# Twelve of 22 inner tiles of a down projection by seven products instead of eight

## The chip, the cores and the metric

The kernel runs on one core of a Trainium2 chip. The core has a matmul engine (TensorE, PE in the profile, with its weight loads as PEld), a vector engine (DVE), a scalar engine (ACT), GpSimd (POOL), and SyncE (SP), which issues most of the DMA transfers. The metric is the time of one execution on the device in microseconds (us); lower is better. The profile is that of one execution.

## The reference

One layer of a bidirectional encoder over a sequence of 1024 positions and width 1024, everything in float32:

```
h = rmsnorm(x)
proj = h @ w_in                      # glu, q, v, z_f, z_b, og, g_a, g_b
a = silu(layernorm(dwconv31(glu))) @ pw_w
o = bidirectional gated scan of q, v, z_f, z_b (8 heads, chunks of 64)
b = (rmsnorm_per_head(o) * norm_w * silu(og)) @ o_w
x = x + (sigmoid(g_a) * a + sigmoid(g_b) * b) @ w_out
h2 = rmsnorm(x)
gate, val = split(h2 @ w_up)         # 1024 -> 2 x 2816
g = silu(dwconv3(gate)) * val
x = x + g @ w_down                   # 2816 -> 1024
out = rmsnorm(x)
```

The change is mostly in `g @ w_down`: 2816 inner channels are 22 tiles of 128. Two other places are touched: the product with `sigmoid(g_a)`, and the last residual addition.

## The kernel before

Activations lie transposed, channels on the 128 partitions and positions along the row, in two halves of 512 positions. So a tile is 128x512 and its products go to one PSUM bank (three banks `mm`, two `sc`, two `tr`, one `ob`). A float32 product is made of three matmuls on float32r parts: `split` (L124) makes the high part by an ACT cast and the low part by a DVE subtraction, and `mm3` (L148 to L150) multiplies high by high, high by low and low by high. So each weight page and each activation tile has to pass through ACT and DVE before PE can use it. Activation parts lie in pages `hx` (32), `hy` and `gx` (16 each), weight parts in `wp` (4 pages) and `wq` (3).

There are two kinds of matmul job. `std_job` takes one column of 128 outputs, loads its raw weights, splits them, and for each half of the sequence accumulates all inner tiles in one `mm` bank, which an `evac` function empties. `pair_job` takes two output columns and two halves as a 2x2 block product and forms it by seven products (Strassen's scheme) instead of eight: sums of weight quadrants and sums of activation quadrants are made first, the products 1, 2, 6, 7, 5, 4, 3 run in this order, products 6, 5 and 3 accumulate on the bank of product 1, product 4 on that of product 7, and three banks in between are copied out by ACT (`copy`, L396). The in-projection and the FFN's up projection go by `pair_job` already. The up projection is 22 such jobs, one for each inner tile: column j of the gate and column j of the value. Its weight sums are made by accumulating DMAs that POOL issues.

The FFN after a job: `evac` (L1561 to L1569) combines products into gate and value; `gated` (L1543 to L1556) does the three-tap convolution, the silu and the product with the value, and stores the tile to DRAM as `d_g[j][half]`. The down projection then reads `d_g` back into `ev` and `tm` tiles, splits them (`load_g`), and goes through the 22 inner tiles in groups of 4, 4, 5, 5 and 4: for each group eight `std_job`s, one for each output column. The first group's evictions copy to the accumulators `xr` (16 tiles, ACT, L1690); the next three add to them (DVE, `add_evac`, L1696). The last group (`last_jobs`, `final_evac`) also adds the residual: it loads a `d_x2` tile, adds `xr` to it (L1731), adds the bank to that, and then `turn_out` transposes the tile, sums squares and applies the gain, and `scale_out` scales and stores.

Earlier, `d_ga` and `d_gb` (the sigmoid gates) are stored by the in-projection. The pointwise product of the convolution branch is a `std_job` for each column whose eviction is an ACT copy into an `ev` tile (three buffers) that is stored to `d_a` (L753, L754). The output product of the scan has `merge` as its eviction: it loads `d_gb`, `d_ga` and `d_a`, multiplies, adds and splits (L1438 to L1441).

The order of the work: PE's instructions run in program order. The generators yield after every two inner tiles, and `Stream.fill(n)` advances a stage by n such pieces. `later(n, f)` queues a chore that is due n pieces on. For the other engines a planner of the compiler orders instructions, except where `pin` keeps the program's order. Each engine, and SP's queue, then works strictly in its order.

Of the kernel before, what the change touches and what calls it, by code (L numbers as in the profile page):

```python
# [10 lines left out]
F32 = mybir.dt.float32  # L11
# [7 lines left out]
P = 128  # L19
# [12 lines left out]
H = 512  # L32
# [15 lines left out]
def tile_hybrid_encoder(  # L48
# [233 lines left out]
    def pair_job(src0, src1, nk, acts, wpool, pool, evac, su=4, first=False, late=False, now=False, direct=False, columns=1, stored=None):  # L282
# [7 lines left out]
        def steps(w):  # L290
# [4 lines left out]
            def add(o, a):  # L295
                if first:
                    V.tensor_tensor(o, o, a, op=ALU.add)
                elif direct:
                    pin(V.tensor_tensor(o, o, a, op=ALU.add))
                else:  # L300
                    G.dma_start(o, a, accum_op=ALU.add)

# [84 lines left out]
        def run(w):  # L387
# [13 lines left out]
            p1 = copy(row)  # L401
# [3 lines left out]
            u2 = copy(row)  # L405
            yield from product(7, col)
            p7 = copy(col)
# [120 lines left out]
    d_us = [dp.tile([P, 4, ND // 2 * P], F32, name=f"d_us_{n}") for n in range(3)]  # L528

# [519 lines left out]

    def pw_col(i):  # L1050
        return w_cols(conv_pw_w, 0, NCW, i * P)
# [4 lines left out]
    def pw_first():  # L1056
        prep, run = std_job(pw_col(0), NCW, ca_of, store(d_a[0]))
# [8 lines left out]
    rest_jobs += [std_job(pw_col(i), NCW, ca_of, store(d_a[i])) for i in range(1, ND - 2)]  # L1066
    rest_jobs.append(
        duo_job(pw_col(ND - 2), pw_col(ND - 1), NCW, ca_of, store(d_a[ND - 2]), store(d_a[ND - 1]))
# [365 lines left out]
    def merge(i):  # L1434
        def evac(half, acc):
            sb, sa, a = ev(), ev(), tmp()
            for t, src in ((sb, d_gb), (sa, d_ga), (a, d_a)):
                nc.sync.dma_start(t, src[i][half])  # L1438
            V.tensor_tensor(a, a, sa, op=ALU.mult)
# [53 lines left out]

    h2 = {i: [] for i in range(1, 8)}
# [42 lines left out]
    def ffn_job(j):  # L1537
        val = [None, None]

        def gated(hf):  # L1540
            o, g = hf * H, gp[j % 2]
# [14 lines left out]
            nc.sync.dma_start(d_g[j][hf], val[hf])  # L1556

        def evac(e, half, x0, x1=None, op=None):
# [4 lines left out]
            g = gp[j % 2]  # L1563
# [18 lines left out]
            now=j == 0,  # L1582
            stored=sums_of(d_us[j], ND // 2) if j < len(d_us) else None,
# [75 lines left out]
    groups = [4, 4, 5, 5, 4]  # L1659
    landing = itertools.cycle([ev] * 3 + [tmp] * 4)  # L1660
    gs, jobs = [], []

    def load_g(f, half):

        t = next(landing)()
        nc.sync.dma_start(t, d_g[f][half])
        while len(gs) <= f:
            gs.append([None, None])

        def parts():  # L1670
            gs[f][half] = split(g_page(), g_page(), t, V, True)

        return parts

    s_ffn.fill(14 * (NF - 1) - s_ffn.count)
    for f in range(groups[0]):
# [9 lines left out]
    xr = [[page(fd, "xr", 2 * ND) for _ in range(2)] for _ in range(ND)]  # L1686

# [6 lines left out]
    def add_evac(i):  # L1694
        def f(half, acc):
            V.tensor_tensor(xr[i][half], acc, xr[i][half], op=ALU.add)  # L1696

        return f

    def down_jobs(f0, n, evac):  # L1700
        return [
            std_job(
                w_cols(ffn_w_down, f0 * P, n, i * P), n, lambda k, half: gs[f0 + k][half], evac(i)
            )
            for i in range(ND)
        ]

    def last_jobs(f0, evac):
# [3 lines left out]
        def job(i, half):  # L1712
# [7 lines left out]
            return prep, std_job(None, 4, lambda k, h: gs[f0 + k][h], evac(i), (half,), 1)[1]  # L1720
# [16 lines left out]
    def turn_out(i, half):  # L1737

        t = xr[i][half]
        if i == 0:  # L1740
            out_sum.append(fd.tile([P, ND, 4], F32, tag="os", name=nm("os"), bufs=2))
            out_y.append(fd.tile([P, 4, D], F32, tag="y", name=nm("y"), bufs=2))
        ss, y = out_sum[half], out_y[half]
# [3 lines left out]
        for c in range(4):  # L1747
            junk = fd.tile([P, P], F32, tag="oj", name=nm("oj"), bufs=2)
            A.activation(
                junk, b[:, c * P : (c + 1) * P], AF.Square, accum_out=ss[:, i, c : c + 1]  # L1750
# [23 lines left out]
    def scale_out(half, c):  # L1774
# [12 lines left out]
    out_sum, out_y, out_r = [], [], []  # L1787
    fnw = fd.tile([P, D], F32, name="fnw")
    f0 = 0
    nc.sync.dma_start(  # L1790
        fnw, bass.AP(tensor=final_norm_w.tensor, offset=final_norm_w.offset, ap=[[0, P], [1, D]])
    )
    for n, group in enumerate(groups):
        last = n == len(groups) - 1
        if last:
            st = Stream(run_jobs(last_jobs(f0, final_evac)))
            st.fill(4 * ND + 3)
            finish(0)
            st.drain()
            advance_chores(1 << 10)  # L1800
            finish(1)
        else:
            st = Stream(run_jobs(down_jobs(f0, group, add_evac if n else first_evac)))
            st.fill(12)
            for f in range(f0 + group, f0 + group + groups[n + 1]):
                for half in range(2):
                    later(4, load_g(f, half))
                    st.fill(2)
            st.drain()
            advance_chores(1 << 10)  # L1810
        f0 += group
# [33 lines left out]
```

## Time and profile before

| | us |
|---|---|
| median of 3 runs | 1760.56 |
| lowest and highest | 1758.67, 1764.92 |
| profiled execution | 1763.45 |
| its span | 1761.7 |
| PE busy | 1727.4 (98%) |
| DVE busy | 1207.7 (69%) |
| ACT busy | 808.8 (46%) |
| POOL busy | 156.3 (9%) |

The span is the time from the first to the last recorded instruction; the execution's own time is 1.75 us longer. The stages, by the start of their instructions: in-projection and convolution up to about 480 us, the rest of the in-projection and the scan up to about 830, pointwise product up to about 900, scan output and merge up to about 980, `w_out` up to about 1070, up projection up to about 1505, down projection from there (its first eviction starts at 1508.7, the last one of the fourth group at 1700.0), last group and final norm to the end.

In rows of groups, the part after the bar is busy time, mean ns of one, then the time that the engine was idle just before, and what ended it. In rows of the timeline: start, duration, engine, line, operation, tiles, and in brackets the idle time before with its releaser. In rows of windows: the window, its length, busy time of each engine, the granted clock of PE (1.00 is full speed), the busy share of the DMA engines, and GB/s. Matmul records overlap: the time from one to the next is shorter than the duration of one.

### The profile page before, as it was taken

The page shows a single profiled execution, that of the slowest core. Times are in us where ns is not written, and L with a number is a line of the kernel's source. Part 1 is how long each engine was busy: PE and PEld are TensorE (multiplying, and loading weights), DVE is VectorE, ACT ScalarE, POOL GpSimd, SP SyncE. Part 2 cuts the span into 40 slices and gives each one's busy share as a digit, 9 for nine tenths or more (in the row PEclk, how much of TensorE's full clock was granted, in tenths as well). Part 3 has the DMA queues.
Part 4 walks back from the last instruction along what each step waited for, and adds up shares of the span by engine and source line. Part 5 has one row for each costly group of instructions (what it writes and reads, how often), then busy time and mean ns, then how long its engine had stood idle before and what let it go on. Part 6 is the DMA issues. An engine that isn't in the chain of part 4 may idle for free. (4 is left out here: it accounts for less than half of the span.)

```text
span 1761.7 us, 30307 instructions
## 1 busy us (share of the span) xinstructions
PE 1727.4 (98%) x11878; PEld 1421.6 (81%) x11878; DVE 1207.7 (69%) x1845; ACT 808.8 (46%) x1518; POOL 156.3 (9%) x168
## 2 busy tenths in 40 slices
PE   8999999999999999999999999999999999999997
PEld 6878888887888788888878787888888888888885
DVE  5599999646678878887366566766676667444455
ACT  7444443334476677776542345443443344422223
POOL 2201111100000000000000002111111111000000
PEclk9999999999999999999999999999999999999999
DMA  8778878855663433435489765667766775534233
GB/s 286 241 164 190 195 180 210 201 146 188 207 194 107 122 116 119 140 107 195 127 264 293 229 207 186 159 146 150 152 147 145 148 143 144 160 100 126 73 92 137
DMA packets 333413, 292.33 MB, mean 166 GB/s; under 512 B 24526, under 2 KB 251606, under 8 KB 333270
## 3 DMA queue, kind: packets, MB, share of 16 engines
q1 hardware_dynamic: 281558, 255.78, 46.6%
q0 software_dynamic: 42496, 33.56, 13.4%
q10 hardware_dynamic: 9216, 1.05, 0.4%
q8 instruction: 93, 1.52, 0.4%
q14 instruction: 50, 0.41, 0.1%
HBM read 192.55 MB, written 79.95 MB: 155 GB/s over the span
## 5 line engine op out<-in xcount | busy, mean ns | idle before, releaser
L148 PE MATMUL mm<-hx,wp 128*128 128x512 f32 x1144 | 457.1, 400 | 3.0 <-ACT tm L799 1.7
L150 PE MATMUL mm<-hx,wp 128*128 128x512 f32 x1144 | 446.9, 391 | 2.1 <-DVE wp L124 2.0
L149 PE MATMUL mm<-hx,wp 128*128 128x512 f32 x1144 | 445.9, 390 | 0.0
L124 ACT CAST wp<-wr 128x1024 fp32r<-128x1024 f32 (+2 forms) x171 | 162.1, 949 | 360.2 <-PE mm L149 204.4
L150 PEld LDWEIGHTS mm<-hx,wp 128*128 128x128 f32 x1144 | 214.7, 188 | 50.6 <-DVE wp L124 4.8
L148 PEld LDWEIGHTS mm<-hx,wp 128*128 128x128 f32 x1144 | 214.9, 188 | 49.6 <-DVE ev L748 2.4
L149 PEld LDWEIGHTS mm<-hx,wp 128*128 128x128 f32 x1144 | 215.1, 188 | 42.2 <-issue 0.7
L124 DVE TENSOR_TENSOR wp<-wr,wp 128x1024 fp32r<-128x1024 f32 (+2 forms) x169 | 185.9, 1101 | 87.4 <-ACT wp L124 86.4
L987 DVE SCALAR_TENSOR_TENSOR acc<-gl,v_b,acc 128x1024 f32<-128x1024 f32 x120 | 149.0, 1279 | 0.4
L1696 DVE TENSOR_TENSOR xr<-mm,xr 128x512 f32<-128x512 f32 x48 | 33.2, 691 | 72.8 <-PE mm L150 72.8
L1083 DVE TENSOR_TENSOR qF<-qF,tb 128x512 f32<-128x512 f32 x96 | 64.9, 684 | 14.2 <-ACT A L1115 14.1
L396 ACT COPY su<-mm 128x512 f32<-128x512 f32 x82 | 47.6, 580 | 57.5 <-PE mm L150 57.3
L124 ACT CAST wq<-sw 128x1024 fp32r<-128x1024 f32 x41 | 43.1, 1051 | 58.3 <-PE mm L149 45.5
L1083 DVE TENSOR_TENSOR kG<-kG,tb 128x512 f32<-128x512 f32 x96 | 65.3, 683 | 4.9 <-PE sc L1217 4.6
L1545 DVE SCALAR_TENSOR_TENSOR tm<-gp,v_a,tm 128x512 f32<-128x512 f32 x88 | 65.9, 749 | 3.9 <-ACT tm L1543 2.0
L148 PE MATMUL mm<-hy,wp 128*128 128x512 f32 x164 | 64.5, 393 | 0.0
L148 PE MATMUL tr<-hx,wp 128*128 128x512 f32 x164 | 64.3, 392 | 0.0
L149 PE MATMUL mm<-hy,wp 128*128 128x512 f32 x164 | 64.2, 392 | 0.0
L148 PE MATMUL sc<-hy,wq 128*128 128x512 f32 x164 | 64.2, 392 | 0.0
L150 PE MATMUL sc<-hy,wq 128*128 128x512 f32 x164 | 64.2, 391 | 0.0
L150 PE MATMUL tr<-hx,wp 128*128 128x512 f32 x164 | 63.8, 389 | 0.0
L149 PE MATMUL tr<-hx,wp 128*128 128x512 f32 x164 | 63.8, 389 | 0.0
(354 smaller groups left out, 3419.5 us busy)
## 6 DMA issues: line engine op xcount, KB each, us to landing
wr<-in_w_in_dram SPq DMA_DIRECT2D x48, 512.0 KB, 4.3
wr<-in_ffn_w_up_dram SPq DMA_DIRECT2D x22, 512.0 KB, 6.0
d_g<-ft SPq DMA_DIRECT2D x44, 256.0 KB, 3.8
sw<-in_w_in_dram SPq DMA_DIRECT2D x38, 256.0 KB
sw<-in_ffn_w_up_dram SPq DMA_DIRECT2D x38, 256.0 KB, 3.7
sw<-in_ffn_w_up_dram POOLq DMA_DIRECT2D x19, 512.0 KB, 8.7
wr<-sw POOLq DMA_DIRECT2D x32, 256.0 KB, 3.8
wr<-wr POOLq DMA_DIRECT2D x32, 256.0 KB, 4.2
```

The costliest lines, as they stand in the source:

```text
L124: parts = A.copy(hi, src), eng.tensor_tensor(lo, src, hi.bitcast(F32), op=ALU.subtract)
L148: T.matmul(acc, whi[:, k, :], ahi, start=first, stop=False, skip_group_check=again)
L149: T.matmul(acc, whi[:, k, :], alo, start=False, stop=False, skip_group_check=again)
L150: T.matmul(acc, wlo[:, k, :], ahi, start=False, stop=last, skip_group_check=again)
L396: A.copy(t, acc)
L987: V.scalar_tensor_tensor(acc, g[:, k : k + S], tap(k), acc, op0=ALU.mult, op1=ALU.add)
L1083: V.tensor_tensor(o, a, b, op=op)
L1545: V.scalar_tensor_tensor(c, g[:, o + k : o + k + H], vec("fdw", k * NF + j), c, op0=ALU.mult, op1=ALU.add,)
L1696: V.tensor_tensor(xr[i][half], acc, xr[i][half], op=ALU.add)
```

## The change

1. **Down projection.** Inner tiles 0 to 5 stay dense, as one group of six. Tiles 6 to 17 go as two sets of six by seven products: a set's six tiles are two rows of three, the output columns i and i+4 are the two columns of the block, the two halves of the sequence are the other side. Four jobs (i = 0 to 3) make a set; each has seven products of three inner tiles, 63 matmuls. Tiles 18 to 21 stay as the last group.
2. **Weights of those jobs.** `pair_job` gets an argument `take`. With it the raw weights come by two loads of 384 KB into pages `sr` (four buffers), DVE makes four sums of 128x384, and ACT and DVE split three pages of 768 columns and one of 384.
3. **Eviction of the three intermediate banks.** Instead of an ACT copy, `take` has DVE add the bank to (or subtract from) the accumulator `xr` into a page; the final evictions put the results into `xr`.
4. **Pair differences.** The seven products need b12 - b22, b11 - b12, a third difference and a sum of the activation tiles. `g_sums` makes these in the up projection, four DVE operations and four stores (`d_gc`) for each of six pairs of inner tiles, as chores due 6 to 9 pieces later. `ffn_order` orders the up projection's jobs so that the tiles of a pair follow each other. Six stores to `d_g` that nobody reads are dropped. The down projection loads 21 tiles for a set instead of 12.
5. **Gate product.** `gated_a` loads the `d_ga` tile at the pointwise product and multiplies the bank by it (DVE) in place of the ACT copy; `merge` loads two tiles instead of three and has one multiplication fewer.
6. **Residual.** In the last set, POOL issues an accumulating DMA from `d_x2` into `xr` after each final eviction (16 of them); `final_evac` is one DVE addition, with no load.
7. The final norm's gain is loaded, and its small tiles are allocated, ahead of the down projection; the stages of the down projection form one stream (`fill_to`) with a table of places at which tiles are loaded.

```diff
+            if take is not None:
...
+                rows, other = raw(src0), raw(src1)
+                yield 4
+                w[1], w[2] = both(rows, None)
+                col = raw()
+                plus(col[:, :nk], rows[:, :nk], other[:, :nk])
+                plus(col[:, nk:], other[:, :nk], other[:, nk:])
+                yield 2
+                plus(rows[:, :nk], rows[:, :nk], col[:, nk:])
+                plus(rows[:, nk:], rows[:, nk:], rows[:, :nk])
+                yield 4
+                w[7], w[5] = both(col, pool)
+                yield 3
+                w[6], w[3] = both(rows, None)
+                yield 3
+                one = w_page(2 * nk, pool)
+                w[4] = split(one[:, :nk], one[:, nk:], other[:, nk:], V, late)
+                return
...
-            def copy(acc):
+            def copy(acc, i):
                 t = page(pool, "su", su)
-                A.copy(t, acc)
+                if take is not None:
+                    take(i, t, acc)
+                else:
+                    A.copy(t, acc)
                 return t
...
+    def gated_a(i):
+        def evac(half, acc):
+            t = ev()
+            nc.sync.dma_start(t, d_ga[i][half])
+            V.tensor_tensor(t, acc, t, op=ALU.mult)
+            nc.sync.dma_start(d_a[i][half], t)
...
-            sb, sa, a = ev(), ev(), tmp()
-            for t, src in ((sb, d_gb), (sa, d_ga), (a, d_a)):
+            sb, a = ev(), tmp()
+            for t, src in ((sb, d_gb), (a, d_a)):
                 nc.sync.dma_start(t, src[i][half])
-            V.tensor_tensor(a, a, sa, op=ALU.mult)
             V.tensor_tensor(sb, acc, sb, op=ALU.mult)
...
+    def g_sums(f, b11, b12, b21, b22):
+        t7 = []
+
+        def make(i, o, a, b, op=ALU.subtract):
+            V.tensor_tensor(o, a, b, op=op)
+            nc.sync.dma_start(d_gc[f][i - 4], o)
+
+        def first():
+            t7.append(page(up, "ft", 8))
+            make(7, t7[0], b12, b22)
+
+        later(6, first)
+        later(7, lambda: make(5, b12, b11, b12))
+        later(8, lambda: make(6, b11, t7[0], b11))
+        later(9, lambda: make(4, b21, b11, b21, ALU.add))
...
-            nc.sync.dma_start(d_g[j][hf], val[hf])
+            if not (hf and j in b12_only):
+                nc.sync.dma_start(d_g[j][hf], val[hf])
...
-    groups = [4, 4, 5, 5, 4]
...
+    def seven_evac(i, last):
+        def out_of(e, half):
+            return xr[i + e * ND // 2][half]
+
+        def take(n, t, acc):
+            at, op = {1: ((0, 0), ALU.add), 6: ((1, 0), ALU.subtract), 7: ((1, 1), ALU.add)}[n]
+            V.tensor_tensor(t, acc, out_of(*at), op=op)
+
+        def f(e, half, x0, x1=None, op=ALU.add):
+            t = out_of(e, half)
+            V.tensor_tensor(t, x0, t if x1 is None else x1, op=op)
+            if last:
+                o = i + e * ND // 2
+                G.dma_start(t, d_x2[o][half], accum_op=ALU.add)
+
+        return f, take
...
         def f(half, acc):
-            x2 = load(d_x2[i][half])
-            V.tensor_tensor(x2, x2, xr[i][half], op=ALU.add)
-            V.tensor_tensor(xr[i][half], acc, x2, op=ALU.add)
+            V.tensor_tensor(xr[i][half], acc, xr[i][half], op=ALU.add)
...
+    for s in range(SEVENS):
+        todo = [(FIRST + 2 * NS * s, i, k) for i in PRODUCTS for k in range(NS)]
+        if s == 0:
+            at = [12 + 2 * n for n in range(12)] + [starts[0] - 2 + n for n in range(9)]
         else:
-            st = Stream(run_jobs(down_jobs(f0, group, add_evac if n else first_evac)))
...
+            at = [starts[s] - 36 + 6 * n for n in range(NS)]
+            at += [
+                starts[s] - per_seven - 2 + per_seven // 7 * n + max(0, k - 1)
+                for n in range(1, 7)
+                for k in range(NS)
+            ]
+        for n, key in zip(at, todo):
+            fill_to(n)
+            later(4, load_seven(*key))
```

More of the change, by code (lines that the diff above doesn't have):

```diff
@@ L1657, in g_page, with load_part, parts, load_seven @@
         return hx() if next(n_g) == 0 else page(fd, "gx", 16, F32R)
-    groups = [4, 4, 5, 5, 4]
     landing = itertools.cycle([ev] * 3 + [tmp] * 4)
-    gs, jobs = [], []
-    def load_g(f, half):
[L1665 to L1673, printed above, removed]
+    gs = {}
+    def load_part(key, src):
+        t = next(landing)()
+        nc.sync.dma_start(t, src)
+        def parts():
+            gs[key] = split(g_page(), g_page(), t, V, True)
+        return parts
+    def load_g(f, half):
+        return load_part((f, half), d_g[f][half])
+    def load_seven(f0, i, k):
+        f = f0 + k
+        src = {1: d_g[f][0], 2: d_g[f + NS][0], 3: d_g[f + NS][1]}
+        return load_part((f0, i, k), src[i] if i < 4 else d_gc[f][i - 4])
     s_ffn.fill(14 * (NF - 1) - s_ffn.count)
-    for f in range(groups[0]):
+    for f in range(FIRST):
         for half in range(2):
@@ L1785, in scale_out @@
         nc.sync.dma_start(out[0, n * P : (n + 1) * P, :], y[:, c, :])
[L1787 to L1801, printed above, removed]
-        else:
-            st = Stream(run_jobs(down_jobs(f0, group, add_evac if n else first_evac)))
[L1804 to L1811, printed above, removed]
+    out_y, out_r = [], []
```

129 lines of the change are left out of this document (105 added, 24 removed).

## The prediction

> **What bounds the kernel now.** I read the page's first two parts, then the waits of PE, then windows by stage.
>
> ```profile
> span 1761.7 us, 30307 instructions
> PE 1727.4 (98%) x11878; PEld 1421.6 (81%) x11878; DVE 1207.7 (69%) x1845; ACT 808.8 (46%) x1518; POOL 156.3 (9%) x168
> ...
> PE   8999999999999999999999999999999999999997
> ...
> PEclk9999999999999999999999999999999999999999
> ```
>
> TensorE (PE) is busy for 98% of the span, in every slice but the first and the last, at an undisturbed granted clock. The kernel is bound by the number of matmuls, so a cut of matmuls counts in full as long as nothing makes PE wait. Where it waits now:
>
> ```profile
> PE sc L1217 <- DVE qF L1083: 4.2, 7, 1.0
> PE mm L150 <- DVE wp L124: 3.4, 5, 1.4
> PE mm L606 <- DMA xt<-in_x_dram: 2.6, 1, 2.6
> ```
>
> The largest single releaser is worth 4.2 us of 1761.7. Next the stages that the change touches: the merge (900 to 980 us), the up projection (1100 to 1490), the down projection's dense groups (1510 to 1700), and the end.
>
> ```profile
> core 0: us, PE busy (x) PEld busy (x) DVE busy (x) ACT busy (x) POOL busy (x), PEclk, DMA share, GB/s
> 900.00:980.00 80.00, 79.02 (x347) 64.79 (x347) 54.51 (x79) 19.18 (x27) 0.00 (x0) 1.00 0.96 294
> 1100.00:1490.00 390.00, 389.78 (x1695) 317.79 (x1694) 263.89 (x345) 159.18 (x226) 63.37 (x57) 1.00 0.69 149
> 1510.00:1550.00 40.00, 40.00 (x178) 33.14 (x177) 11.28 (x17) 16.01 (x29) 0.00 (x0) 1.00 0.44 132
> 1550.00:1700.00 150.00, 150.00 (x664) 124.20 (x663) 71.82 (x108) 34.98 (x58) 0.00 (x0) 1.00 0.33 100
> 1730.00:1762.00 32.00, 19.44 (x99) 15.62 (x97) 15.44 (x28) 12.47 (x69) 1.01 (x1) 0.86 0.42 156
> ```
>
> In the down projection PE never waits (150.00 busy of 150.00) and DVE is busy 48% of the time. The up projection has DVE at 68%. Only the merge is near another bound: its DMA engines are 96% busy, and PE is idle 0.98 us there. The last 32 us hold 12.6 us without PE.
>
> The step of one matmul follows from DVE, which evicts one bank after every 12 matmuls of a group of four tiles:
>
> ```profile
> 1551.22 0.69 DVE L1696 TENSOR_TENSOR xr<-mm,xr 128x512 f32<-128x512 f32 x1 [2.03 <-PE mm L150]
> 1551.83 0.68 DVE L124 TENSOR_TENSOR wp<-wr,wp 128x512 fp32r<-128x512 f32 x1
> 1553.94 0.69 DVE L1696 TENSOR_TENSOR xr<-mm,xr 128x512 f32<-128x512 f32 x1 [1.43 <-PE mm L150]
> 1556.66 0.69 DVE L1696 TENSOR_TENSOR xr<-mm,xr 128x512 f32<-128x512 f32 x1 [2.03 <-PE mm L150]
> ```
>
> 1556.66 - 1551.22 = 5.44 us for two banks, so 2.72 us for 12 matmuls and 0.2267 us for each. The rows also give DVE's own step: an operation of 0.69 us starts 0.61 us after the one before it when both are queued (1551.22, 1551.83).
>
> **The change part by part.** The durations used:
>
> ```profile
> L1696 DVE TENSOR_TENSOR xr<-mm,xr 128x512 f32<-128x512 f32 x48 | 33.2, 691 | 72.8 <-PE mm L150 72.8
> L124 DVE TENSOR_TENSOR wp<-wr,wp 128x640 fp32r<-128x640 f32 x16 | 13.1, 817 | 0.0
> L124 DVE TENSOR_TENSOR hx<-tm,hx 128x512 fp32r<-128x512 f32 x18 | 12.0, 686 | 4.1 <-ACT hx L124 4.1
> L124 ACT CAST wp<-wr 128x640 fp32r<-128x640 f32 x16 | 11.7, 732 | 78.2 <-PE mm L149 78.2
> L124 ACT CAST hx<-tm 128x512 fp32r<-128x512 f32 x18 | 10.5, 617 | 2.1 <-DMA tm<-d_g 2.1
> L1690 ACT COPY xr<-mm 128x512 f32<-128x512 f32 x16 | 9.2, 584 | 9.7 <-PE mm L150 9.7
> L124 DVE TENSOR_TENSOR wp<-wr,wp 128x1024 fp32r<-128x1024 f32 x40 | 48.9, 1222 | 34.0 <-ACT wp L124 34.0
> ```
>
> *Matmuls.* A set of six inner tiles takes 8 columns x 2 halves x 6 x 3 = 288 matmuls now. By seven products it is 4 jobs x 7 products x 3 tiles x 3 = 252. Two sets: 72 fewer, 72 x 0.2267 = **-16.3 us**. That is the most that the change can give on PE; everything else is what eats into it.
>
> *DVE load of a seven job.* A job lasts 63 x 0.2267 = 14.3 us, a product 2.04 us. DVE has in it seven evictions (7 x 0.69), four sums of raw weights 128x384, three weight splits of 128x768 and one of 128x384. Between the rows (686 ns for 512 columns, 817 for 640, 1222 for 1024) I interpolate 0.95 us for 768 and extrapolate 0.55 for 384: 4.8 + 2.2 + 2.9 + 0.6 = 10.5 us, 73% of the job against 48% now. On average it fits. But a dense eviction has two spare banks behind it, whereas here products 1, 6 and 7 are evicted by DVE and product 6 goes into product 1's bank, 5 on 6, 4 on 7. Between the end of one and the start of the one that accumulates on its bank lies one other product: 2.04 us. DVE takes its work in order, so what is queued in front of such an eviction counts.
>
> I laid the rows' durations along the changed program's issue order, job by job.
> - First seven job: ahead of the eviction of product 6 stand the next job's weight split (whose cast waits for product 2 to end, to have its page free), two sums, two splits of gated activations (the g tiles) and a 384 split. The eviction ends about 10.0 us into the job; product 5 wants the bank at 8.13. **+1.9 us**; 1 to 3.5 by which DVE step (0.61 or 0.69) holds.
> - From set 1 to set 2: 18 of the 21 g tiles of set 2 are split in the last job of set 1 and the first of set 2. Nine splits of 0.69 on top of 10.5 is 16.7 us of DVE work in 14.3 us, and PE slips: 0.45 at product 6's eviction, 0.3 at 7's, 0.8 at product 1's of the next job, and 2.2 where product 6 needs the low part of its weights. **+3.8 us**; 6 with the 0.69 step. Range 2 to 8.
> - The other six jobs: the eviction of product 6 has some 0.15 us to spare, and one job has an additional split in front of it (0.45). **+0.7 us**, 0 to 3. This margin is the thinnest of all: 0.2 us more per job is 1.2 us.
>
> ACT has the casts in a job, three of 768 columns (some 0.84 us by the step from 617 for 512 to 732 for 640), one of 384, g casts, and none of the evictions: 3 to 9 us of 14.3. It has room throughout. The raw weights of a job come in two loads of 384 KB:
>
> ```profile
> wr<-in_ffn_w_down_dram SPq DMA_DIRECT2D x16, 320.0 KB, 3.5
> ev<-d_g SPq DMA_DIRECT2D x20, 256.0 KB, 3.4
> d_g<-ft SPq DMA_DIRECT2D x44, 256.0 KB, 3.8
> wr<-sw POOLq DMA_DIRECT2D x32, 256.0 KB, 3.8
> ```
>
> 320 KB land in 3.5 us, so 384 KB in about 4.2; they are issued most of a job ahead into four buffers. The DMA share is 0.33 there, and 18 more g loads of 256 KB (3.4 us each) in over 110 us change nothing. Cost 0; if the cover were gone, product 1 of a job would start late by part of 4 us.
>
> *Pair differences in the up projection.* 24 more DVE operations of 128x512 and 18 more stores (24 new, 6 dropped) of 256 KB, in six of the 22 jobs. 24 x 0.69 = 16.5 us against 390 - 263.9 = 126 us that DVE is idle in that stage. SP gets three more stores per pair job and POOL none; DMA was at 0.69. What is late next is the chain that ends at product 6:
>
> ```profile
> 1250.31 0.69 DVE L1569 TENSOR_TENSOR gp<-mm,rs 128x512 f32<-128x512 f32 x1 [2.06 <-PE mm L150]
> 1252.61 1.05 ACT L124 CAST wp<-wr 128x1024 fp32r<-128x1024 f32 x1 [6.95 <-DMA wr<-wr]
> 1253.69 1.23 DVE L124 TENSOR_TENSOR wp<-wr,wp 128x1024 fp32r<-128x1024 f32 x1 [2.69 <-ACT wp L124]
> 1255.56 0.39 PE L148 MATMUL mm<-hx,wp 128*128 128x512 f32 x1
> ```
>
> DVE is free from 1251.0 to 1253.69, waits for ACT's cast, which waits for the summed weights, and is done 0.64 us before product 6 starts. The new operations stand behind evictions, one after each of several, so that an eviction or split is at most one operation (0.61) later; the summing DMAs (3.8 us) may start 0.5 us later because they follow a split. 0.64 covers that, barely. **+0.5 us**, 0 to 4. At the change to the down projection, 12 g tiles are split in the last up job instead of 8, with 0.3 to 0.5 us to spare in my tally: **+0.3 us**, 0 to 1.5.
>
> *Gate product at the pointwise product, and the merge.*
>
> ```profile
> L754 SPq DMA_DIRECT2D d_a<-ev x16: 319/320/366, 830.2 to 897.5; - x16
> ...
> DMA to landing us min/median/max: 2.0/2.0/4.3
> L1439 DVE TENSOR_TENSOR tm<-tm,ev 128x512 f32<-128x512 f32 x8 | 5.5, 689 | 10.2 <-DMA ev<-d_ga 7.1 <-DMA tm<-d_a 3.1
> ev<-d_ga SPq DMA_DIRECT2D x16, 256.0 KB, 3.6
> 984.79 0.50 PE L150 MATMUL mm<-mg,wp 128*128 128x512 f32 x1 [1.38 <-DVE wp L124]
> ```
>
> The 16 copies by ACT (0.58) become DVE multiplies that need a load of d_ga first: 3.6 us to land while the DMA engines are 96% busy. Three buffers go round load, multiply 0.7, store 2.0, about 6.3 to 6.8 us, against 3 x 2.72 = 8.2 us in which PE makes three banks. Queued behind the waiting multiply on DVE are the hx and wp splits; on SP, behind a load that waits for a buffer, other loads. Two spare banks of PE cover up to 5.4 us of delay. Cost 0, up to +3. The merge then has one load and one multiply fewer for each of 16 evictions: 16 x 256 KB = 4.2 MB less at 294 GB/s is 14 us less of DMA work in the stage that DMA fills, and moves it to one with room. PE loses only 0.98 us in the stage and 1.38 after it, so the gain is bounded by these: **-0.7 us**, -2.4 to +3.
>
> *Residual.* 16 loads of d_x2 and 16 DVE adds leave the last stage, and POOL issues 16 adding DMAs of 256 KB in the last four seven jobs (3.8 us as the existing adding DMAs). The last evictions come 10 us or more later. PE was full from 1700 to 1730 anyway; the final 12.6 us are transposes, norm and stores, which the change keeps. **0**; if an adding DMA were late, only its eviction (two spare banks) would be.
>
> **Sum:** -16.3 + 1.9 + 3.8 + 0.7 + 0.5 + 0.3 - 0.7 = **-9.8 us**. The profiled execution took 1763.45 us (span 1761.7), which gives 1753.7; it lies 2.9 us above the median of the runs, 1760.56. Against the median I forecast 1760.6 - 9.8 = **1751 us**.
>
> **Clock.** The granted clock stood at 1.00 in all windows above but the last, 0.86, where PE has 12.6 us of gaps; the pauses of up to 2.6 us in the waits did not lower it to a visible degree. The Trainium skill ("TensorE: Matmul & The Clock Gate", Part 1: The HAM clock gate) says that an idle window of about 3.4 us halves the clock until PE has been busy again for as long. The rows agree with it as far as they go. By that rule the stalls of this sum, none over 2.2 us, cost no more than themselves; if those at the change of sets merged to one of 4 us, it would add an estimated 1.7 us.
>
> **Rivals.**
> A. *DVE holds, no stalls appear.* For it: 73% load, and my margins are tenths of a microsecond. Against it: nine splits in a job that has room for five. Time: 1760.6 - 16.3 - 0.7 + 0.8 = 1744.
> B. *DVE becomes the bound of the seven jobs.* Each of the three evictions that stand between two products pays 0.5 us more than I put (an eviction from the bank's end to PE's start has semaphore time that my tally leaves out): 8 jobs x 3 x 0.5 = 12 less the spare 0.15 each, some 8 us. Then -9.8 + 8 = -1.8: 1759, no measurable change. For it: every margin counted is below 0.5 us. Against: the gaps in the DVE rows above (2.03 between operations) show evictions starting promptly.
> C. *Slower: the loads of d_ga block the pointwise stage.* SP's queue is in order and the ev tiles have three buffers; when a load waits for a buffer whose store has not landed, everything behind it, weights for PE included, waits too. A cycle of c us for three buffers against the 8.2 us of three banks costs (c - 8.2)/3 for each of 16 evictions. It decides from c = 10.0 us, where it costs 9.8 and cancels the gain; loads of 3.6 us that stand 4 us in SP's queue, with stores at their slowest, 4.3, make about 12, which costs 20 us: 1771. For it: that slowest landing, and the loads stand in one queue with the weights. Against: the median landing of 2.0 us.
> D. *The summed weights of the up projection are late.* 0.64 us of margin; if the six pair jobs each lose 1.5 us: 9 us, 1760.
>
> **How the numbers follow.** Forecast (1747 to 1755): 0.46. A: 0.16. B, with D: 0.22, of which about two thirds within 0.3% (5.3 us, about what a measurement of this kernel can tell from no change) and the rest faster. C and a B so strong that it passes the whole gain: 0.16, all slower. Faster: 0.46 + 0.16 + 0.07 = 0.69; same 0.15; slower 0.16. The range leaves out the upper part of C and a little below A: 1744 to 1765.
>
> **What would show it.** The PE row has 72 matmuls fewer, and busy time falls by about 16 us. Waits of PE on DVE's eviction (mm L-line of the new take) and on wp splits appear in the seven jobs, 5 to 7 us in all, the first of them in the first job and most at the change of sets. No wait of PE at the pointwise product; the merge's DMA share falls well below 0.96. The up stage ends within 1 us of where it did. I am wrong if PE waits in every seven job (B), if PE idles around 840 to 900 us (C), or if the up stage is 5 us longer (D).

## The result and the profile after

The changed kernel takes 1755.86 us (median of 6 runs, 1754.85 to 1757.8) against 1761.99 for the kernel before in the same comparison: 6.1 us less, a ratio of 0.9964, 95% interval 0.9951 to 0.9977. The profiled execution took 1754.85 us, span 1753.0; the span before was 1761.7, so the two profiles, which are one execution each, differ by 8.7 us. They differ by more than the medians because the one before (1763.45 us) lies 1.5 us above its median and the one after 1.0 us below. The forecast was 1751 us and -9.8.

The first parts of the page after:

```profile
span 1753.0 us, 30378 instructions
PE 1715.2 (98%) x11806; PEld 1409.3 (80%) x11806; DVE 1253.1 (71%) x1919; ACT 819.9 (47%) x1528; POOL 170.0 (10%) x184
...
DVE  5599999746678888788556466676667777548864
...
PEclk9999999999999999999999999999999999999998
```

DVE's row before, for comparison:

```profile
DVE  5599999646678878887366566766676667444455
```

PE has 72 matmuls fewer, as counted, but its busy time fell by 12.2 us, not 16.3, and DVE now is at eight tenths in two slices of the down projection where it was at four. The waits of PE from 820 us to the end:

```profile
PE mm L150 <- DVE wp L124: 2.2, 2, 1.9
PE mm L148 <- DVE su L1791: 1.8, 2, 1.4
PE sc L1865 <- DVE xr L1852: 1.8, 2, 0.9
PE tr L1865 <- DVE xr L1852: 0.9, 1, 0.9
PE mm L148 <- ACT hx L124: 0.8, 2, 0.5
PE ob L585 <- POOL tm L605: 0.7, 1, 0.7
PE mm L148 <- ACT gx L124: 0.5, 1, 0.5
PE mm L149 <- DVE hx L124: 0.5, 2, 0.2
```

The first two rows are the waits that were forecast: the weight's low part (1.87 us) and the eviction `take` (L1791; 1.41 and 0.43 us). In the third and fourth the transposes of the last group wait for its evictions, three times some 0.9 us. The last of the three, at 1741.1 us, was there before as well; the two at 1699.3 and 1703.6 are new and were not forecast. By windows, merge first, then the change of sets, then the start of the last group:

```profile
900.00:980.00 80.00, 79.25 (x348) 64.61 (x347) 51.05 (x73) 20.75 (x29) 0.00 (x0) 1.00 0.89 279
...
1611.00:1643.00 32.00, 29.67 (x128) 23.38 (x127) 29.66 (x48) 15.62 (x26) 2.10 (x3) 1.00 0.67 201
...
1690.00:1720.00 30.00, 27.64 (x136) 21.69 (x135) 14.47 (x24) 12.58 (x70) 1.03 (x1) 1.00 0.20 54
```

The start of the last group before:

```profile
1700.00:1730.00 30.00, 30.00 (x151) 24.79 (x150) 17.59 (x31) 10.09 (x68) 1.03 (x1) 1.00 0.30 79
```

At the change of sets DVE is busy 29.66 of 32 us and PE loses 2.33 us. At the start of the last group, where before PE was full, it loses 2.36 us while DVE is busy less than half of the time.

The stages from the timelines, as differences after minus before. A combination is one of the DVE operations that make gate and value out of the seven products. The down projection's start is set back from its regular evictions: 1502.3 before, 1501.4 after.

| stretch | before | after | difference |
|---|---|---|---|
| start to the first combination of the up projection | 1079.6 | 1079.3 | -0.3 |
| up projection, first to last combination | 419.9 | 419.4 | -0.5 |
| from there to the down projection's start | 2.8 | 2.7 | -0.1 |
| down projection to the start of the last group | 195.8 | 184.8 | -11.0 (-16.3 + 5.1 lost, rounded) |
| last group, start to last eviction | 50.8 | 54.1 | +3.3 |
| behind it | 12.8 | 12.7 | -0.1 |

The 5.1 us of the fourth row are 1.7 in the first seven job (from its first to its last eviction 13.95 us, where six products of 2.04 make 12.24) and 3.4 in the two jobs around the change of sets (31.96 us where two jobs make 28.56). In the other five jobs PE is busy for 14.28 of 14.28 us: nothing is lost. At the change of sets PE waits twice, for the eviction of product 1 of the second of these jobs and for the low part of product 6's weights there:

```profile
1630.60 0.47 PE L148 MATMUL mm<-hx,wp 128*128 128x512 f32 x1 [0.43 <-DVE su L1791]
1633.17 0.50 PE L150 MATMUL mm<-hx,wp 128*128 128x512 f32 x1 [1.87 <-DVE wp L124]
```

A wait of PE costs more than its idle time, since matmuls otherwise overlap (they last 0.39 us and start every 0.2267). From one start of a matmul to the next, less the usual 0.2267 us, these two places cost 0.7 and 2.15 us; two places without an idle time, behind the evictions of products 6 and 7 of the first of them, cost 0.2 and 0.3.

So two questions: where the 3.3 us of the last group come from, and whether the 5.1 are DVE's load.

### The profile page after: what moved, and what is told of

Same layout as the page of the kernel before. It is cut to its first block, busy times and chain, and to the rows that moved or that the text cites. A ratio compares the mean times of both kernels' runs of the same rounds, so it can differ in the third digit from the quotient of the medians.

```text
span 1753.0 us, 30378 instructions
## 1 busy us (share of the span) xinstructions
PE 1715.2 (98%) x11806; PEld 1409.3 (80%) x11806; DVE 1253.1 (71%) x1919; ACT 819.9 (47%) x1528; POOL 170.0 (10%) x184
## 5 line engine op out<-in xcount | busy, mean ns | idle before, releaser
L148 PE MATMUL mm<-hx,wp 128*128 128x512 f32 x1068 | 428.2, 401 | 4.2 <-ACT tm L835 2.3
L150 PE MATMUL mm<-hx,wp 128*128 128x512 f32 x1068 | 418.0, 391 | 2.3 <-DVE wp L124 2.2
L149 PE MATMUL mm<-hx,wp 128*128 128x512 f32 x1068 | 417.1, 391 | 0.5 <-DVE hx L124 0.5
L124 ACT CAST wp<-wr 128x1024 fp32r<-128x1024 f32 (+2 forms) x147 | 147.3, 1003 | 261.8 <-PE mm L149 115.0
L148 PEld LDWEIGHTS mm<-hx,wp 128*128 128x128 f32 x1068 | 201.0, 188 | 48.3 <-ACT tm L835 2.8
L150 PEld LDWEIGHTS mm<-hx,wp 128*128 128x128 f32 x1068 | 200.8, 188 | 47.6 <-DVE wp L124 4.7
L149 PEld LDWEIGHTS mm<-hx,wp 128*128 128x128 f32 x1068 | 201.2, 188 | 40.5 <-DVE hx L124 1.2
L124 DVE TENSOR_TENSOR wp<-wr,wp 128x1024 fp32r<-128x1024 f32 (+2 forms) x145 | 169.6, 1170 | 75.0 <-ACT wp L124 68.4
L148 PE MATMUL tr<-hx,wp 128*128 128x512 f32 x180 | 70.5, 392 | 0.0
L150 PE MATMUL tr<-hx,wp 128*128 128x512 f32 x180 | 70.1, 389 | 0.0
L149 PE MATMUL tr<-hx,wp 128*128 128x512 f32 x180 | 70.0, 389 | 0.0
L148 PE MATMUL sc<-hy,wq 128*128 128x512 f32 x164 | 64.2, 392 | 0.0
L150 PE MATMUL sc<-hy,wq 128*128 128x512 f32 x164 | 64.2, 391 | 0.0
L149 PE MATMUL sc<-hy,wq 128*128 128x512 f32 x164 | 63.8, 389 | 0.0
```

Of the source, the lines that this page charges most:

```text
L124: parts = A.copy(hi, src), eng.tensor_tensor(lo, src, hi.bitcast(F32), op=ALU.subtract)
L148: T.matmul(acc, whi[:, k, :], ahi, start=first, stop=False, skip_group_check=again)
L149: T.matmul(acc, whi[:, k, :], alo, start=False, stop=False, skip_group_check=again)
L150: T.matmul(acc, wlo[:, k, :], ahi, start=False, stop=last, skip_group_check=again)
```

## The experiments

All ratios are against the kernel before, on the same chip, with their 95% intervals. Many of the intervals below overlap that of the changed kernel (0.9951 to 0.9977); there the times alone do not tell two runs apart, and what is said of a place rests on one profile of each run.

**The last group.** Up to 1702 us ACT waits there for nothing but the group's weights. ACT and the `wr` tile after:

```profile
1691.93 0.62 ACT L124 CAST gx<-wr 128x512 fp32r<-128x512 f32 x1 [14.87 <-DMA wr<-in_ffn_w_down_dram]
```
```profile
L135 SPq DMA_DIRECT2D wr<-in_ffn_w_down_dram x6: 367/368/380, 1686.1 to 1698.7; - x6
L124 ACT CAST gx<-wr x6: 617/620/622, 1691.9 to 1701.6; 128x512 fp32r<-128x512 f32 x6
...
L124 ACT CAST hx<-wr x2: 622/623/624, 1675.8 to 1676.4; 128x512 fp32r<-128x512 f32 x2
L124 DVE TENSOR_TENSOR hx<-wr,hx x2: 687/688/689, 1685.4 to 1686.0; 128x512 fp32r<-128x512 f32 x2
```

The casts of the first two columns are done at 1677, but DVE makes the low parts only at 1685.4, behind the last job's evictions; only then are the two `wr` buffers free, and six loads start at 1686.1, where PE starts the last group. Before, all eight loads of the last group were issued ahead of its start at 1698.1:

```profile
L135 SPq DMA_DIRECT2D wr<-in_ffn_w_down_dram x8: 367/368/384, 1679.2 to 1695.8; - x8
```

How a late weight reaches PE is seen on DVE: the split of the weight, which waits for ACT's cast, stands in front of an eviction, and PE's transposes wait for that eviction.

```profile
1697.95 0.69 DVE L124 TENSOR_TENSOR gx<-wr,gx 128x512 fp32r<-128x512 f32 x1 [0.42 <-ACT gx L124]
1698.56 0.68 DVE L1852 TENSOR_TENSOR xr<-mm,xr 128x512 f32<-128x512 f32 x1
```
```profile
1699.30 0.66 PE L1865 MATMUL tr<-ident,xr 128*128 128x128 f32 x4 [0.88 <-DVE xr L1852]
```

The rival is that the residual's adding DMAs, issued at the same place, crowd these loads. Two runs bear on it.

Early weights: five of the loads go to free `ev` and `tm` tiles.

```diff
+                    raw = early_w.pop(i, None)
...
+    def load_w(i):
+        early_w[i] = next(landing)().rearrange("p (k e) -> p k e", k=4)
+        nc.sync.dma_start(early_w[i], w_cols(ffn_w_down, LAST0 * P, 4, i * P))
...
     for f in range(LAST0, NF):
...
+            if (f, half) in ((NF - 2, 1), (NF - 1, 0)):
+                fill_to(n - 2)
+                load_w(2 + (f == NF - 1))
+    fill_to(n - 2)
+    for i in (4, 5, 6):
+        load_w(i)
     st.drain()
```

> The changed kernel, with the raw weights of columns 2 to 6 of the last group loaded into the free ev and tm tiles, issued before the last seven job ends, instead of through the two wr buffers. In the changed kernel PE needs 54.1 us from the start of the last group (1686.2) to its last eviction (1740.3); before, 50.8. Theory 1 (these loads are late because a wr buffer comes free only when DVE has split it, behind the evictions of the last seven job): 51 us, no wait of PE between 1690 and 1705, time 3 us below the changed kernel. Theory 2 (the adding DMAs of the residual crowd out the weight loads at this place): the loads are still slow, 53 to 54 us, time unchanged.

Measured: 0.9946 (0.9933 to 0.9958), 1752.47 us. One of the five loads is issued at 1635.9, the others from 1668.5 to 1679.5, and PE is full behind the last seven job:

```profile
1687.00:1701.00 14.00, 14.00 (x69) 11.57 (x68) 6.35 (x10) 3.94 (x25) 0.86 (x1) 1.00 0.40 69
```

The last group takes 50.7 us, as before the change: theory 1.

Residual as before:

```diff
-            if last:
-                o = i + e * ND // 2
-                G.dma_start(t, d_x2[o][half], accum_op=ALU.add)
...
-            V.tensor_tensor(xr[i][half], acc, xr[i][half], op=ALU.add)
+            x2 = load(d_x2[i][half])
+            V.tensor_tensor(x2, x2, xr[i][half], op=ALU.add)
+            V.tensor_tensor(xr[i][half], acc, x2, op=ALU.add)
```

> The changed kernel with the residual as before: no adding DMAs, 16 loads of d_x2 and 16 DVE additions in the last group. Theory 1 (weights late by their buffers): the last group still takes 54 us or a little more, since the 16 loads join SP's queue; time unchanged or up to 2 us longer. Theory 2 (adding DMAs crowd the weight loads): about 51 us, time 3 us shorter.

Measured: 0.9963 (0.9951 to 0.9976), the changed kernel's own. In its profile the last group takes 52.8 us, between the two theories: the first load of the pair is cast 4.5 us after its issue (1686.3, 1690.9), with the adding DMAs 5.9 us (1686.1, 1691.9). So the adding DMAs may have a part in it, some 1.3 of the 3.3 us by one profile each, in a run that also puts the 16 loads and additions back. The late issue is the cause without which there is no loss: with early weights the adding DMAs are still there, and the last group takes 50.7 us. As ways of adding the residual, the two cannot be told apart by the time.

**The gate product alone**, on the kernel before (the `gated_a` and `merge` hunks of the diff).

> The kernel before with one part of the change: the gate product at the pointwise product's eviction, one load and one multiplication fewer in the merge. My prediction's sum gives -0.7 us against before. Theory: no new wait of PE at 830 to 900 us, and PE's idle time from 900 to 1070 us falls from 2.5 us to under 1; time 0 to 2 us shorter. Rival C of the prediction: PE idle by several us at 840 to 900, time longer by up to 10 us.

Measured: 0.9993 (0.9984 to 1.0002). From the first store of `d_a` to the first combination of the up projection it is 248.1 us against 249.4. PE's idle time from 900 to 1070 us falls from 2.53 us to 0.67, as in the theory. PE's waits from 820 us on have no entry at the pointwise product, and the 2.8 us on `wp` (four waits before) are 0.3:

```profile
PE mm L149 <- DVE hx L124: 0.5, 2, 0.3
PE mm L150 <- DVE wp L124: 0.3, 1, 0.3
```

The gain is about 1.3 us in the profile, too small for the time to show. Nothing here speaks for rival C.

**The pair differences alone**, on the kernel before (the `g_sums`, `ffn_order` and `ffn_job` hunks, with every `d_g` stored), and the same without the stores of the differences.

> The kernel before with the pair differences alone: the up projection's jobs in the changed order, 24 more DVE operations and their 24 stores, which nothing reads; the down projection as before. My sum has +0.5 us for them. Theory: from the first to the last combination of the up projection (419.9 us before) within 1 us of that, time 0 to 1 us longer. Rival D of the prediction: the summed weights are late in six jobs, 5 to 9 us longer.

> The run with the pair differences alone, without their 24 stores: the 24 DVE operations stay. The run with stores had an up projection of 424.5 us between its markers (419.9 before) and was 0.2% slower. Theory 1 (the stores' traffic makes the summed weights land later): back to 419 to 421 us, time as before. Theory 2 (the DVE operations themselves delay the chain): still 423 to 425 us, time 2 to 4 us longer than before.

Measured: 1.0018 (1.0009 to 1.0027) with the stores, 1.0005 (0.9996 to 1.0013) without. The up projection takes 424.5 and 418.8 us. So the 24 DVE operations cost nothing that can be seen; with the stores there is sometimes a loss. By the times alone the two runs are not clearly apart (their intervals overlap from 1.0009 to 1.0013). The place, in the run with stores, is ACT's wait for the summed weights, then PE's wait for the copy that stands behind it on ACT; last, the two windows there:

```profile
ACT wp L124 <- DMA wr<-wr: 9.8, 1, 9.8
```
```profile
1431.12 0.50 PE L148 MATMUL mm<-hx,wp 128*128 128x512 f32 x1 [1.77 <-ACT su L396]
```
```profile
1428.63:1432.05 3.42, 1.61 (x7) 0.71 (x6) 1.43 (x2) 2.51 (x4) 1.22 (x1) 1.00 0.27 76
1432.05:1435.46 3.41, 3.41 (x9) 2.65 (x10) 3.28 (x6) 1.79 (x4) 0.36 (x1) 0.50 0.61 142
```

The sums by adding DMAs land late once, PE idles 1.77 us, and then for 3.41 us the granted clock is 0.50, which costs another 1.7 us; the two are most of the 4.6 us (424.5 against 419.9). That the stores make the sums late is argued from the run without them, not shown. The changed kernel has the same chain, with 18 more stores instead of 24. Of the nine profiles here that have these stores and their readers, seven (the changed kernel's among them) show 418.7 to 420.2 us for the up projection and two 422.3 and 422.6: a loss of 0 to 3 us that differs from one execution to the next.

**DVE's load at the change of sets.** First by POOL (`pool_keys` holds every second tile, and the condition picks set 2):

```diff
+            eng = G if len(key) == 3 and key[0] > FIRST and key[1:] in pool_keys else V
-            gs[key] = split(g_page(), g_page(), t, V, True)
+            gs[key] = split(g_page(), g_page(), t, eng, True)
```

> The changed kernel with 10 of the 21 low parts of set 2's g tiles (every second one) made by POOL instead of DVE. Theory (DVE's load of 16 to 17 us in a 14.3 us job makes PE slip at the change of sets): DVE is relieved of 6 us over those two jobs, the two waits there (0.43 and 1.87 us) and the small ones around them shrink from 3.4 us in all to under 1; time 2 to 3 us shorter. Rival (the casts on ACT or the pages' release set the pace there): the waits stay, time unchanged. A POOL operation of this kind takes 1.39 us in the profile, so a third result is that POOL is late itself and the time grows.

Measured: 0.9976 (0.9967 to 0.9986), by the ratio 2 us slower than the changed kernel; in its profile the two jobs around the change of sets lose 5.8 us instead of 3.4. It does not answer the question, because DVE itself got slower. DVE's sums in this run, 1618 to 1640 us, then POOL's operations there:

```profile
L312 DVE TENSOR_TENSOR sr<-sr 128x384 f32<-128x384 f32 x3 | 3.5, 1165 | 0.0
L124 DVE TENSOR_TENSOR wp<-sr,wp 128x768 fp32r<-128x768 f32 x3 | 3.3, 1105 | 0.6 <-ACT wp L124 0.6
L312 DVE TENSOR_TENSOR sr<-sr,sr 128x384 f32<-128x384 f32 x3 | 3.2, 1071 | 0.0
L124 DVE TENSOR_TENSOR hx<-tm,hx 128x512 fp32r<-128x512 f32 x2 | 2.9, 1466 | 0.0
...
L1798 DVE TENSOR_TENSOR xr<-tr,su 128x512 f32<-128x512 f32 x2 | 1.4, 684 | 0.1
```
```profile
L124 POOL TENSOR_TENSOR hx<-tm,hx 128x512 fp32r<-128x512 f32 x3 | 4.8, 1607 | 7.7 <-DVE wq L124 4.3 <-ACT hx L124 3.4
```

The sums of 128x384 take 1165 and 1071 ns where the changed kernel has 552 and 554, and a split 1466 where it has 688. An eviction, with one input in PSUM, keeps its 684 (687 in the changed kernel). The Trainium skill ("SBUF — State Buffer", Who interferes with whom) says that a DVE instruction with two SBUF inputs contends with a GpSimd instruction that reads SBUF, and that one with at most one SBUF input does not; these rows agree.

So the operations were taken away instead of moved: ten low parts are not made, and `gs[key]` is the high part twice (those tiles therefore count twice in the output, not, as the expectation says, without their small terms).

```diff
+            if key not in no_lo:
...
+            hi, _ = g_page(), g_page()
+            pin(A.copy(hi, t))
+            gs[key] = hi, hi
```

> The changed kernel without the low parts of 10 of set 2's 21 g tiles (the high part is used in their place, so that the result lacks those small terms; PE's work is the same). DVE has 10 x 0.61 = 6 us less to do around the change of sets, and no other engine gets it. Theory (DVE's load there): the 3.4 us that the two jobs around the change lose now shrink to under 1, time 2 to 3 us shorter. Rival (casts or pages set the pace): the loss and the time stay. It also tells whether the POOL run was slow because POOL was late, or because DVE's operations were stretched while POOL worked.

Measured: 0.9948 (0.9934 to 0.9962), by the ratio 2.8 us less than the changed kernel. The two jobs around the change of sets take 29.15 us, 0.6 more than two jobs need, where 3.4 were lost:

```profile
1609.60:1638.70 29.10, 28.89 (x127) 23.48 (x126) 24.66 (x39) 15.37 (x27) 2.33 (x3) 1.00 0.75 220
```

With DVE at 24.66 of 29.1 us, PE loses 0.2 us there. Only DVE's operations were taken away, and the casts on ACT stayed: DVE's load is the cause.

**Toward a faster version.** With early weights, the first group's tiles loaded half by half, and the last nine splits of set 1 ahead of the first seven job (early entry):

```diff
-    for f in range(FIRST):
-        for half in range(2):
+    for half in range(2):
+        for f in range(FIRST):
...
-            at = [12 + 2 * n for n in range(12)] + [starts[0] - 2 + n for n in range(9)]
+            at = [12 + 2 * n for n in range(12)] + [starts[0] - 7 + n // 2 for n in range(9)]
```

> The early weights of the last group, and the first group's g tiles loaded half by half, so that pages come free one half sooner and the last nine splits of set 1 stand ahead of the first seven job instead of in it. Theory (the first job's loss of 1.7 us comes from the splits queued in front of its evictions): that job loses under 0.3 us, time 1.5 us below the run with early weights alone. Rival: the loss only moves, to the first product's start, and the time stays.

Measured: 0.9942 (0.9930 to 0.9954), 1751.16 us; the 1.5 us against early weights alone (0.9946) do not show in the time. The first seven job lost nothing (14.3 us), as the theory has it. But in its profile the change of sets lost 5.0 us instead of 3.4, with the same two waits, 0.43 and 1.87 us. The windows there:

```profile
1626.68:1630.09 3.41, 1.11 (x4) 0.57 (x4) 3.41 (x6) 2.98 (x5) 0.86 (x1) 1.00 0.96 303
1630.09:1633.50 3.41, 3.41 (x9) 2.64 (x9) 2.44 (x5) 0.00 (x0) 0.00 (x0) 0.50 1.06 298
```

Behind the two waits, 2.3 us of idle time in 3.41, the granted clock is 0.50 for 3.41 us. That costs 3.41 x 0.50 = 1.7 us, about the difference. In the changed kernel (0.43 and 1.87) and in the run with early weights alone (0.4 and 1.9) two such waits left the clock at 1.00; the last section shows why.

Set 2's late tiles spread over two jobs:

```diff
-                starts[s] - per_seven - 2 + per_seven // 7 * n + max(0, k - 1)
+                starts[s] - per_seven + 4 * (n - 1) + k
```

> The run with early weights and early entry, and set 2's 18 late g tiles split one at a time over two jobs (four pieces for each product's three tiles) instead of bunched over one. DVE's work in the two jobs is the same, 32 us in 28.6. Theory by place (what stands in front of an eviction counts): the loss at the change of sets falls from 3.4 to 1 or 2 us. Theory by sum (32 against 28.6): it stays at 3.4 us.

Measured: 0.9936 (0.9922 to 0.9949), 1750.45 us; the loss at the change of sets is 2.55 us (31.11 for two jobs), with waits of at most 0.93. That lies between the two theories; most of the loss stays, with the same DVE work (busy 29.61 us here, 29.66 in the changed kernel), so it goes with the sum more than with the place. The first seven job loses 0.5 us in this profile, though it has the early entry too. Against the run before it the time can't be told apart. It has the lowest ratio of all runs, and is the only one whose interval lies below that of the changed kernel.

The weight sums off DVE, by adding DMAs as in the up projection (the new `take` block in `steps` left out, so that the general path is taken), without and with the spread:

> The run with early weights and early entry, with the weight sums of the seven jobs made by adding DMAs that POOL issues, as in the up projection, instead of by four DVE sums of 128x384 for each job: DVE has 4 x 0.47 = 1.9 us less in each job of 14.3, and POOL reads no tile itself. At the change of sets that makes 28.2 us of DVE work in 28.6. Theory by sum (DVE's total in the two jobs): the loss of 3.3 us there falls under 1, time 2 to 3 us shorter. Rival (as in the POOL run): what POOL does at the same time stretches DVE's operations, or the sums land late; then new waits on wp, time the same or longer.

> The same with set 2's late tiles spread by four pieces a product. Theory by sum: no further gain, within 0.5 us of the run without the spread; theory by place: 1 us shorter.

Measured: 1.0073 (1.0056 to 1.0090) and 1.0066 (1.0053 to 1.0079), some 23 us slower than the runs that they build on. The rival: the sums land late. ACT's waits from 1560 to 1700 us without the spread, and what PE waits for:

```profile
ACT wp L124 <- DMA wr<-wr: 36.3, 6, 8.0
```
```profile
PE mm L148 <- DVE su L1762: 9.5, 3, 5.8
PE mm L148 <- ACT hx L124: 6.8, 2, 4.7
```

The three adding DMAs of a job go one after the other and take 7.2, 3.0 and 4.4 us (medians from issue to landing), 14.6 in all: too long for a job of 14.3 us, where the up projection has 19. DVE's splits wait for ACT's casts (23.7 us in this stretch), and what stands behind them in order on ACT and DVE is late with them, the evictions among it.

## Why the prediction was right or wrong

- *Direction and bound.* Right: PE was the bound, 72 matmuls fewer are worth 16.3 us, and part of it was eaten. Measured -6.1 against -9.8: 1755.86 us is inside the range (1744 to 1765), at the upper edge of the band that the forecast itself had (1747 to 1755). That it came so near is in part luck: the sum left out 3.3 us in the last group, and its terms for the other jobs, the pair differences and the entry were 2.1 us too large together.
- *First seven job, +1.9.* 1.7 measured, at the place named (product 5 behind the eviction of product 6, 1.41 us as a wait). Early entry removed it in one profile and left 0.5 us in the next.
- *Change of sets, +3.8.* 3.4 measured, and its four terms are found one by one: 0.2 at product 6's eviction (forecast 0.45), 0.3 at product 7's (0.3), 0.7 at product 1's of the next job (0.8; the wait of 0.43), and 2.15 at the low part of product 6's weights (2.2; the wait of 1.87). The run without ten low parts shows that DVE's load is the cause.
- *The other six jobs, +0.7.* There are five of them, eight less the first and the two at the change of sets. Nothing was lost in them: DVE was busy for 9.8 to 11.6 us of their 14.28.
- *Pair differences, +0.5, and the entry, +0.3.* -0.5 and -0.1 in the profile. The operations cost nothing that can be seen; with the stores 0 to 3 us are lost by execution, inside the bounds given, by the chain named (the summed weights). What I put down to a split ahead of the summing DMAs is, in the one profile followed, their late landing.
- *Gate product, -0.7.* About -1.3 in the profile of that part alone; with all parts, 248.1 us from the first store of `d_a` to the up projection, the same. The merge's DMA share fell from 0.96 to 0.89 only.
- *"Residual: 0. PE was full from 1700 to 1730 anyway."* This step failed: +3.3 us in the last group. I had argued from the loads and additions that leave the stage and had not followed what prepares its weights: two `wr` buffers, freed by DVE splits that now stand behind the seven jobs' evictions. Before, the eight loads were issued ahead of the group.
- *"By that rule the stalls of this sum, none over 2.2 us, cost no more than themselves."* Wrong in places: a window of the clock need not be idle as a whole, as the last section shows. In the profile after, it happened at the start (from 98.84 us, behind a wait of 2.3 us where before it was 1.7), outside the change, and hides the gate product's gain in the first row of the table.

The terms of the two profiles add up: -16.3 + 5.1 + 3.3 - 0.3 - 0.5 - 0.1 - 0.1 = -8.9, against -8.7 between the spans; the rest is rounding in the marks. The gain by the medians is 6.1 us, with an interval of 4.1 to 8.6.

## What to carry to other kernels

When a stage gets denser on a helper engine, follow also the preparation of the stage behind it: a small ring of buffers that was refilled in the idle time of that engine is refilled late, and the loss shows where nothing was changed. A tally of row durations along the issue order found the stalls of a DVE-bound stretch here to within 0.3 us each, and taking operations away, though the output then differs, tests the cause more cleanly than moving them to another engine, which can slow the first. An engine that has room on average may have none for a burst: here the five jobs with 9.8 to 11.6 us of DVE work in 14.28 lost nothing, the one with 13.6 lost 1.7 us, and the two with 29.7 where two jobs make 28.56 lost 3.4.

## What the runs showed of the hardware that was not expected

Idle times near 2 us can halve PE's clock; whether they do depends on where they lie. The slow stretches ahead of the kernel's end all have a granted clock of 0.50 and last 3.41 us, or twice that, and those of one trace begin a whole number of 3.413 us apart (after: at 98.84 and, at the kernel's end, at 1744.07 us, which is 482 x 3.4133 later). So a trace can be cut into windows of 3.41 us that begin where a slow stretch begins. In the profile after, at the start and at the change of sets:

```profile
95.43:98.84 3.41, 1.23 (x5) 1.05 (x6) 1.24 (x2) 2.03 (x3) 0.00 (x0) 1.00 1.12 346
98.84:102.26 3.42, 3.42 (x9) 2.64 (x8) 2.96 (x5) 1.24 (x2) 0.45 (x3) 0.50 0.41 119
...
1631.43:1634.84 3.41, 1.67 (x7) 1.41 (x8) 3.41 (x7) 1.37 (x3) 0.86 (x1) 1.00 0.92 315
1634.84:1638.25 3.41, 3.41 (x16) 2.82 (x16) 3.41 (x7) 0.00 (x0) 0.00 (x0) 1.00 1.03 284
```

With PE busy for 1.23 us of a window, the next is slow: nine matmuls where the later one has 16. With 1.67 us it is not. The two pairs of windows shown above have 1.61 us (pair differences) and 1.11 us (early entry) ahead of a slow one. With early weights alone the same two waits fall into two windows:

```profile
1629.37:1632.78 3.41, 2.48 (x10) 1.42 (x8) 3.41 (x7) 3.38 (x7) 0.00 (x0) 1.00 0.82 267
1632.78:1636.20 3.42, 2.05 (x9) 1.72 (x10) 3.42 (x6) 0.96 (x2) 0.86 (x1) 1.00 1.00 312
```

In all thirteen profiles, from 20 us on, each window at full clock in which PE was busy for 47% or less (up to 1.61 of 3.42 us) is followed by a slow one, and none with 49% or more (from 1.67 of 3.41) is. Between the two nothing was seen. So a stall of 2 us costs itself, and another 3.41 x 0.50 = 1.7 us where it leaves PE busy for less than about half of one window; where the windows lie differs by execution (one begins at 94.03 us before, at 95.43 after). The rule that the prediction took from the Trainium skill ("TensorE: Matmul & The Clock Gate", Part 1: The HAM clock gate) has an idle window of about 3.4 us for this, and says that the window runs freely. The length and the free-running windows agree with these traces; that the window must be idle does not, since half idle was enough here.

And POOL arithmetic beside DVE can double the time of DVE operations with two SBUF inputs (552 to 1165 ns in the mean), while those that read one input from PSUM keep theirs (684 ns).
